# The last four adaLN units among the last key and query units, in memory of their own

## The chip, the cores and the metric

The kernel runs on one core of a Trainium2 chip. The metric is device time in microseconds (us): the median of the runs. Before the change it is 1355.39 us, the median of three runs from 1355.17 to 1358.63. One further execution was profiled; it took 1356.46 us, and every duration below comes from it.

The engines have these names in the profile: PE is TensorE's matrix product, PEld its weight load, DVE is VectorE, ACT is ScalarE, POOL is GpSimd, and SP is SyncE, which here issues nearly all transfers. "SPq" is SyncE's queue of transfer issues.

## The reference, cut to what matters

One layer of a streaming encoder is applied to a prompt of 1024 frames and to a sample of 32 further frames with caches. All is float32.

```python
mod = silu(c) @ w_ada + b_ada                    # per sequence; 1024 -> 6 * 1024
sh1, sc1, g1, sh2, sc2, g2 = split(mod, 6)
h = x * (1 + sc1) + sh1
mq, mk, mv, mo, mi, mf, fq, fk, fv, ff, gu, gv = split(h @ w_in)
hm = mlstm(...)                                  # 4 heads, chunks of 64
hf = forgetting_attention(fq, fk, fv, ...)       # 8 heads, causal, softmax
hg = gu * (lower_triangle(ws) @ layer_norm(gv) + bs)
mix = concat(hm, hf, hg) @ w_o
x = layer_norm(ALPHA * x + (1 + g1) * mix)
h = x * (1 + sc2) + sh2
y = (silu(h @ w_gate) * (h @ w_up)) @ w_down     # 1024 -> 2816 -> 1024
x = layer_norm(ALPHA * x + (1 + g2) * y)
```

The adaLN vector `mod` has six parts of 1024. The last part, `g2`, is used only where the results of `w_down` are added to `x`.

## The kernel before, in words

Everything is held transposed: features on the 128 partitions, frames along the row. Frames are handled in two groups, the first 512 prompt frames (group 0) and the other 512 with the 32 sample frames (group 1). Precise products are made from a rounded high part and a low part of each operand: `weights` (line 104) loads a raw weight tile, lets ScalarE copy it to `whi` (line 116) and VectorE subtract to `wlo` (line 117); `gemm` (line 123) then makes three matmuls for each 128 rows of depth (lines 129 to 131). Raw weight tiles stand in a ring of RAW = 3 buffers, `whi` and `wlo` in rings of WB = 3.

The adaLN vector is made in 24 units of 256 columns. `ada` (line 183) handles one unit: `ada_load` issues two loads of 512 KB, the halves of its weight; `ada_parts` makes eight small float32 matmuls, each with a 32-column operand on the stationary side, in four groups of 32 output partitions (line 201; the trace has 16 records of them for each unit), half 0 first and half 1 added to it. ScalarE copies the result out (line 204), TensorE transposes it twice (line 209), VectorE sums four strips (line 211), and `ada_end` writes the columns of `mod`. The unit holds one PSUM bank from its first matmul to the reduction. Units 0 to 7 are made with the first projection products in `fm_first`, units 16 to 19 and 8 to 15 among the heads by `more`, in a ring of two buffers named "late". Units 20 to 23 are `g2`.

The middle of the kernel, where the change is, runs in this order in the text of `run`: the output projection of group 0 in two ranges of 256 frames (`wo_range`), where the split weights of its units 3 to 5 are kept for the second range in a pool `pw` of 24 KB for each partition, which is closed then; the first layer norm of group 0 (`ln1`), whose mean and variance use the two PSUM banks of the pool `pt`; the key and query units of the heads 5, 6 and 7 for group 1 (`fm_unit` with `evac_qk`), three weight tiles with two ranges of 272 columns each; the mixers of group 1 (attention, mLSTM and the sample's attention, `mixers`); and the feed-forward tiles of group 0 (`up`, then `down`). PSUM is shared out as three banks `pg` for products, two banks `pt` for transposes and sums, and three more for the mixers. Before, each of the feed-forward tiles 0 to 3 is followed by one adaLN unit, 20 to 23, whose two loads take two of the three raw buffers and whose products stand in a `pg` bank.

The order in which each engine runs its instructions is not that of the text. A planner simulates the program with estimated durations and lets each engine take the instruction that stands first in the text among those that are ready; what comes out is a fixed order for each engine, and each engine, and SyncE's queue of issues too, then follows its order strictly. Some stretches are tied by hand: `tie` (line 98) keeps the mixers' first instructions behind certain feed-forward products. A buffer of a closed pool may be written again when the last reader of the tile that stood there is done.

Of the kernel before, what the change touches and what calls it, by code (L numbers as in the profile page):

```python
# [34 lines left out]
PRE = 5  # L35
# [8 lines left out]
RAW = 3  # L44
# [11 lines left out]
def weave(*parts):  # L56

    parts = list(parts)
    while parts:
        for p in list(parts):  # L60
            if next(p, parts) is parts:
                parts.remove(p)
# [6 lines left out]
class Kernel:  # L69
# [125 lines left out]
    def ada_parts(self, u, raws, ppool, ptag):  # L195
        self.phase = "ada"
        nc = self.nc
        ps = self.t(ppool, [P, 512], F32, ptag)
        for half, raw in enumerate(raws):
            for k in range(4):  # L200
                nc.tensor.matmul(ps[32 * k:32 * k + 32, :256], self.c32[:, 4 * half + k, :],
                                 raw[:, k * 256:(k + 1) * 256], start=half == 0, stop=half == 1)
        a = self.t(self.pada, [P, 256], F32, "adas", 2)
        nc.scalar.copy(a, ps[:, :256])
        yield
        self.phase = "ada"
        pt = ps[:, 256:512]
        for half in range(2):
            nc.tensor.transpose(pt[:, half * P:(half + 1) * P], a[:, half * P:(half + 1) * P], self.ident)
        m = self.t(self.pada, [P, 4], F32, "adam", 2)  # L210
        nc.vector.tensor_reduce(m.rearrange("p (h j) -> p h j", h=2), pt.rearrange(
            "p (h g j) -> p h j g", h=2, g=4)[:, :, 0:2, :], AX.X, ALU.add)
        self.ada_end(u, m)
# [1274 lines left out]
    def run(self):  # L1488
        nc, tc, d = self.nc, self.tc, self.d
        dr = self.pool("dr", space=DRAM)  # L1490
        t = lambda shape, tag: self.t(dr, shape, F32, tag)
# [36 lines left out]
        w2, w3 = d["w_in"], d["w_in_f"]  # L1528
# [91 lines left out]
            del kept[0], kept[1]  # L1620
            weave(self.wo_range(st, *MM[0][1], (2, 6, 7, 3, 4, 5, 0, 1), kept, pw), self.ln1(0, st, *MM[0][0]))
        weave(self.ln1(0, st, *MM[0][1]))
        for h in range(PRE, 8):
            self.fm_unit(w3[1 + h], self.evac_qk(h, True), (1,))
        self.ln1_res(0)
        s1.close()
        s4 = ExitStack()
# [8 lines left out]
        for g, (j0, nj) in enumerate(GROUPS):  # L1636
            if g == WOB:
                s4.close()
                s3.close()
                self.pu, self.utag = self.pool("pu", 3, space=PSUM), "gu"  # L1640
                pb = self.pb = self.pool("pb", side="right")
                weave(self.up(0, j0 + 1, act, pa, MM[0]))
                self.operand(1, pb)
                with tc.issue_after(self.lastz.ins):
                    self.wo_mix(1, self.KORDER[1])
                stb = self.ln_begin(nc.gpsimd)
                self.wo(1, stb, MM[1], nc.vector, pb)
                self.operand(1, pb)

                def norm():  # L1650
                    for a, b in MM[1]:
                        yield from self.ln1(1, stb, a, b)

                self.sums()

                def fill():
                    for j in range(j0 + 2, j0 + nj):
                        self.sums()
                        yield from self.up(0, j, act, pa, MM[0])

                weave(fill(), norm())
                continue
            for j in range(j0 + (g > 0), j0 + nj + (g < last)):
                weave(self.up(0, j, act, pa, WIDE if 0 < j < GROUPS[-1][0] else MM[0]))
                if j < 4:
                    self.ada(20 + j, self.wp, "raw", RAW, self.pg, "g")
            if g == WOB - 1:
                st = self.ln_begin(nc.gpsimd, sum=False)
                self.down(0, g, act, WIDE, st)
            else:  # L1670
                self.down(0, g, act, WIDE)
# [37 lines left out]
        t = self.t(self.pz, [P, 4, n], F32R, "z0", 1)  # L1709
        w = self.last_weights(((t[:, 0], t[:, 1]), (t[:, 2], t[:, 3])), (2, 3))  # L1710
        act2 = dict(act)
        for half, (a, b) in enumerate(LN[1][::-1]):
# [6 lines left out]
            else:  # L1719
                h, l = (self.t(pb, [P, KT * 272], F32R, f"{x}{a}", 1) for x in ("ah", "al"))  # L1720
# [118 lines left out]
```

## Time and profile before

| | |
|---|---|
| median of the runs | 1355.39 us |
| the profiled execution | 1356.46 us, span 1354.7 us |
| TensorE (PE) busy | 1329.9 us, 98% |
| VectorE (DVE) busy | 996.8 us, 74% |
| ScalarE (ACT) busy | 660.3 us, 49% |
| last key and query units | 419.8 to 438.7 us |
| adaLN units 20 to 23 | first products at 451.2, last at 505.2 us |

The span is the time from the first to the last instruction in the trace. A row of the timeline gives the start, the duration, the engine, the line of the kernel, the operation, the tile written and the tiles read (buffer numbers left out), the shape, and how many; brackets at its end give the idle time of the engine before it and what ended it. Matmul ends are modelled and overlap the next matmul, so the distance from one start to the next tells what a matmul takes of TensorE. A tile's name begins with the phase in which it was made: `fm` for key and query units, `up` and `dn` for feed-forward, `fox` for attention, `wo` for the output projection, `lna` for the first norm, `tm` and `head` for earlier projections.

### The profile page before, as it was taken

The page shows a single profiled execution, that of the slowest core. Times are in us where ns is not written, and L with a number is a line of the kernel's source. Part 1 is how long each engine was busy: PE and PEld are TensorE (multiplying, and loading weights), DVE is VectorE, ACT ScalarE, POOL GpSimd, SP SyncE. Part 2 cuts the span into 40 slices and gives each one's busy share as a digit, 9 for nine tenths or more (in the row PEclk, how much of TensorE's full clock was granted, in tenths as well). Part 3 has the DMA queues.
Part 4 walks back from the last instruction along what each step waited for, and adds up shares of the span by engine and source line. Part 5 has one row for each costly group of instructions (what it writes and reads, how often), then busy time and mean ns, then how long its engine had stood idle before and what let it go on. Part 6 is the DMA issues. An engine that isn't in the chain of part 4 may idle for free.

```text
span 1354.7 us, 25087 instructions
## 1 busy us (share of the span) xinstructions
PE 1329.9 (98%) x9402; PEld 1208.8 (89%) x9402; DVE 996.8 (74%) x2106; ACT 660.3 (49%) x1305; POOL 230.5 (17%) x263
## 2 busy tenths in 40 slices
PE   9999999999999999999999999999999999999996
PEld 6798888998999778888888888999999999999995
DVE  4646665678679578686776766778988887988777
ACT  3423555455436554554455355436754553535355
POOL 0101100143236200000000000273710000000341
PEclk9999999999999999999999999999999999999998
DMA  9594665546464865354334333664696858553321
GB/s 360 187 306 152 170 200 176 176 150 196 143 210 133 225 184 162 103 159 133 117 109 133 102 90 96 216 172 127 174 251 162 215 152 217 146 178 125 94 79 67
DMA packets 120088, 221.70 MB, mean 164 GB/s; under 512 B 18708, under 2 KB 63920, under 8 KB 119968
## 3 DMA queue, kind: packets, MB, share of 16 engines
q1 hardware_dynamic: 112736, 207.55, 48.6%
q0 software_dynamic: 6032, 11.94, 5.3%
q8 instruction: 74, 1.21, 0.3%
q10 hardware_dynamic: 1200, 0.62, 0.2%
q14 instruction: 46, 0.38, 0.1%
HBM read 188.13 MB, written 51.85 MB: 177 GB/s over the span
## 4 chain that ended last, share of the span: by engine, by line
PE 86%; DVE 6%; DMA 4%; ACT 2%; issue 1%; SPq 0%; POOL 0%; ACTq 0%; DVEq 0%; POOLq 0%
PE up_g L129 5%; PE up_g L131 5%; PE up_g L130 5%; PE dn_g L129 4%; PE dn_g L131 4%; PE dn_g L130 4%; PE tm_g L397 3%; PE tm_g L399 3%; PE tm_g L398 3%; PE sup_u L129 3%; PE sup_u L131 3%; PE sup_u L130 3%; PE wo_g L130 2%; PE wo_g L131 2%; PE wo_g L129 2%; PE fox_t L932 2%
## 5 line engine op out<-in xcount | busy, mean ns | idle before, releaser
L129 PE MATMUL up_g<-tm_ah,up_whi 128*128 128x512 f32 (+1 forms) x384 | 140.2, 365 | 1.2 <-ACT up_whi L116 0.6
L130 PE MATMUL up_g<-tm_al,up_whi 128*128 128x512 f32 (+1 forms) x384 | 140.6, 366 | 0.0
L131 PE MATMUL up_g<-tm_ah,up_wlo 128*128 128x512 f32 (+1 forms) x384 | 139.8, 364 | 0.5 <-DVE up_wlo L117 0.5
L1357 ACT CAST sup_whi<-sup_raw 128x1024 fp32r<-128x1024 f32 x54 | 56.0, 1048 | 90.1 <-PE dn_u L130 46.3
L116 ACT CAST up_whi<-up_raw 128x1024 fp32r<-128x1024 f32 x50 | 52.5, 1049 | 66.3 <-PE dn_g L130 25.8
L129 PEld LDWEIGHTS up_g<-tm_ah,up_whi 128*128 128x128 f32 x384 | 72.2, 188 | 13.7 <-ACT up_whi L116 1.1
L131 PEld LDWEIGHTS up_g<-tm_ah,up_wlo 128*128 128x128 f32 x384 | 72.3, 188 | 11.4 <-DVE up_wlo L117 1.0
L130 PEld LDWEIGHTS up_g<-tm_al,up_whi 128*128 128x128 f32 x384 | 72.2, 188 | 10.5
L1188 DVE SCALAR_TENSOR_TENSOR wo_z<-dn_g,start_mod,wo_z 128x512 f32<-128x512 f32 (+4 forms) x120 | 60.2, 520 | 21.4 <-PE dn_g L131 20.5
L117 DVE TENSOR_TENSOR up_wlo<-up_raw,up_whi 128x1024 fp32r<-128x1024 f32 x50 | 67.2, 1344 | 11.8 <-ACT up_whi L116 9.8
L1358 DVE TENSOR_TENSOR sup_wlo<-sup_raw,sup_whi 128x1024 fp32r<-128x1024 f32 x54 | 68.0, 1262 | 10.6 <-ACT sup_whi L1357 10.5
L905 ACT ACTIVATE fox_p<-fox_s,fox_fmx 128x384 f32<-128x384 f32 (+2 forms) x96 | 55.1, 578 | 40.0 <-DVE fox_fmx L903 29.0
L131 PE MATMUL dn_g<-up_acth,dn_wlo 128*128 128x512 f32 (+2 forms) x200 | 73.7, 369 | 0.0
L130 PE MATMUL dn_g<-up_actl,dn_whi 128*128 128x512 f32 (+2 forms) x200 | 73.4, 368 | 0.0
L129 PE MATMUL dn_g<-up_acth,dn_whi 128*128 128x512 f32 (+2 forms) x200 | 73.4, 368 | 0.0
L116 ACT CAST dn_whi<-dn_raw 128x1024 fp32r<-128x1024 f32 (+1 forms) x44 | 42.7, 971 | 56.6 <-PE up_g L130 14.3
L900 DVE TENSOR_REDUCE fox_fmx<-fox_s 128x1 f32<-128x384 f32 (+2 forms) x96 | 52.7, 553 | 19.5 <-PE fox_s L897 18.5
L937 ACT CAST fox_pth<-fox_t 128x512 fp32r<-128x512 f32 (+1 forms) x80 | 41.6, 542 | 46.9 <-PE fox_t L932 44.9
L117 DVE TENSOR_TENSOR dn_wlo<-dn_raw,dn_whi 128x1024 fp32r<-128x1024 f32 (+1 forms) x44 | 49.5, 1125 | 16.4 <-ACT dn_whi L116 16.0
L397 PE MATMUL tm_g<-tm_whi,start_h1h 128*128 128x256 f32 (+1 forms) x192 | 55.9, 291 | 1.8 <-DVE tm_traw L468 1.7
L398 PE MATMUL tm_g<-tm_wlo,start_h1h 128*128 128x256 f32 (+1 forms) x192 | 55.8, 291 | 0.0
L399 PE MATMUL tm_g<-tm_whi,start_h1l 128*128 128x256 f32 (+1 forms) x192 | 55.6, 290 | 0.0
(690 smaller groups left out, 4766.7 us busy)
## 6 DMA issues: line engine op xcount, KB each, us to landing
up_raw<-w_gu SPq DMA_DIRECT2D x50, 512.0 KB
dn_raw<-w_dn SPq DMA_DIRECT2D x28, 512.0 KB
ada_late<-w_ada SPq DMA_DIRECT2D x24, 512.0 KB
sup_raw<-w_gu SPq DMA_DIRECT2D x20, 512.0 KB
start_dp<-w_gu SPq DMA_DIRECT2D x19, 512.0 KB
start_dp<-w_gu POOLq DMA_DIRECT2D x19, 512.0 KB, 8.0
wo_raw<-w_o SPq DMA_DIRECT2D x18, 512.0 KB
sup_raw<-start_dp SPq DMA_DIRECT2D x18, 512.0 KB
```

The source lines that it names most:

```text
L116: nc.scalar.copy(hi[:, :w], raw[:, :w])
L117: (eng or nc.vector).tensor_tensor(lo[:, :w], raw[:, :w], f(hi[:, :w]), ALU.subtract)
L129: nc.tensor.matmul(ps, hi, xh(k), start=start and k == 0, stop=False)
L130: nc.tensor.matmul(ps, hi, xl(k), start=False, stop=False)
L131: self.lastmm = nc.tensor.matmul(ps, lo, xh(k), start=False, stop=stop and k == n - 1)
L397: nc.tensor.matmul(ps[:, :ncol], xh, hi, start=k == 0, stop=False)
L398: nc.tensor.matmul(ps[:, :ncol], xh, lo, start=False, stop=False)
L399: nc.tensor.matmul(ps[:, :ncol], xl, hi, start=False, stop=k == 7)
L905: nc.scalar.activation(pr[:, lo:hi], banks[x][:, :hi - lo], AF.Exp, bias=mxs[:, 0:1], accum_out=sums[:, x:x + 1])
L1188: self.lastz = self.nc.vector.scalar_tensor_tensor(z[:, m, x:y], ps[:, x - a:y - a], g[i], z[:, m, x:y], ALU.mult, ALU.add)
L1357: nc.scalar.copy(h, x)
L1358: tt(l, x, f(h), ALU.subtract)
```

## The change

The four units 20 to 23 leave the feed-forward tiles. Units 20 and 21 stand behind the key and query unit of head 5, unit 22 behind that of head 6, and unit 23 behind that of head 7. Their loads go to a pool `pq` of six buffers "late", 24 KB for each partition, in the memory that `pw` had; their products stand in the two banks of `pt`. And for all units from 8 on, half 1, which is loaded last, is now multiplied first.

```diff
-        for half, raw in enumerate(raws):
+        for i, half in enumerate((0, 1) if ptag == "t" and u < 8 else (1, 0)):
             for k in range(4):
                 nc.tensor.matmul(ps[32 * k:32 * k + 32, :256], self.c32[:, 4 * half + k, :],
-                                 raw[:, k * 256:(k + 1) * 256], start=half == 0, stop=half == 1)
+                                 raws[half][:, k * 256:(k + 1) * 256], start=i == 0, stop=i == 1)
...
-        for h in range(PRE, 8):
-            self.fm_unit(w3[1 + h], self.evac_qk(h, True), (1,))
+        with ExitStack() as s7:
+            pq = self.pool("pq", ctx=s7)
+            for u, h in enumerate(range(PRE, 8)):
+                self.fm_unit(w3[1 + h], self.evac_qk(h, True), (1,))
+                for u in (20, 21) if u == 0 else (21 + u,):
+                    self.ada(u, pq, "late", 6, self.pt, "t")
         self.ln1_res(0)
...
                 weave(self.up(0, j, act, pa, WIDE if 0 < j < GROUPS[-1][0] else MM[0]))
-                if j < 4:
-                    self.ada(20 + j, self.wp, "raw", RAW, self.pg, "g")
```

## The prediction

> **What bounds the kernel now.** I read the page first (span, busy shares, the chain), then the busy time by stretches around the change, then TensorE's own rows in the stretch where the four units now stand.
>
> ```profile
> span 1354.7 us, 25087 instructions
> ```
> ```profile
> PE 1329.9 (98%) x9402; PEld 1208.8 (89%) x9402; DVE 996.8 (74%) x2106; ACT 660.3 (49%) x1305; POOL 230.5 (17%) x263
> ```
> ```profile
> PE 86%; DVE 6%; DMA 4%; ACT 2%; issue 1%; SPq 0%; POOL 0%; ACTq 0%; DVEq 0%; POOLq 0%
> ```
>
> TensorE is busy 98% of the span and holds 86% of the chain that ended last. So an edit is worth what it takes from TensorE's own work or from TensorE's waits, and nothing else. The stretches (first column is the window in us, then its length, busy time of each engine, granted clock, DMA share, GB/s):
>
> ```profile
> 408.00:426.00 18.00, 18.00 (x153) 18.00 (x152) 18.00 (x33) 10.85 (x22) 13.32 (x9) 1.00 0.19 58
> 426.00:439.00 13.00, 13.00 (x103) 12.90 (x103) 11.09 (x21) 9.47 (x21) 5.79 (x5) 1.00 0.77 222
> 439.00:470.00 31.00, 29.25 (x194) 23.85 (x193) 18.02 (x36) 17.56 (x41) 8.75 (x10) 1.00 0.81 216
> 470.00:505.00 35.00, 33.94 (x213) 25.95 (x211) 23.07 (x55) 17.51 (x36) 0.18 (x1) 1.00 0.65 190
> 505.00:560.00 55.00, 55.00 (x321) 45.01 (x321) 42.37 (x92) 28.04 (x62) 1.19 (x3) 1.00 0.52 153
> ```
>
> The last key and query units run at about 420 to 439 us, where TensorE has no idle time. The first feed-forward tiles run from 439, and there TensorE is idle 31 - 29.25 = 1.75 us up to 470 and 35 - 33.94 = 1.06 us up to 505, together 2.81. After that it is full again. That is the whole idle time that can be won near the change.
>
> **The change part by part.** First what the four units do to the tiles they stand between. These are TensorE's waits from 439 to 470 us (start, duration, the idle time before and what ended it in brackets):
>
> ```profile
> 448.19 0.38 PE L129 MATMUL up_g<-tm_ah,up_whi 128*128 128x256 f32 x1 [0.59 <-DVE up_sil L1288]
> ...
> 467.79 0.50 PE L129 MATMUL up_g<-tm_ah,up_whi 128*128 128x512 f32 x1 [0.63 <-ACT up_whi L116]
> ...
> 469.05 0.50 PE L131 MATMUL up_g<-tm_ah,up_wlo 128*128 128x512 f32 x1 [0.53 <-DVE up_wlo L117]
> ```
>
> They add up to 1.75, all that is idle there. The second and third are one late weight tile. Its way back, in SyncE's queue and on ScalarE:
>
> ```profile
> 458.28 1.67 SPq L86 DMA_DIRECT2D ada_raw<-w_ada  x2
> 460.04 0.38 SPq L86 DMA_DIRECT2D up_raw<-w_gu  x1
> ```
> ```profile
> 466.69 1.04 ACT L116 CAST up_whi<-up_raw 128x1024 fp32r<-128x1024 f32 x1 [0.57 <-DMA up_raw<-w_gu]
> ```
>
> The load of the feed-forward weight goes out directly behind two adaLN loads, which use two of the three "raw" buffers that it needs too. ScalarE then waits for it, and TensorE waits for ScalarE and VectorE. With the adaLN loads gone from this ring and this queue, the load goes out at least 460.04 - 458.28 = 1.76 us sooner, which covers 0.63 + 0.53 = 1.16. Term one: -1.16, between 0 (if the ring turns no sooner) and -1.16. What is late next is the softmax of the attention, and TensorE has feed-forward products to do meanwhile.
>
> Second, the products. One unit is 8 small matmuls (16 records); here three of the four:
>
> ```profile
> 451.21 0.63 PE L201 MATMUL ada_g<-ada_raw,start_c 128*32 128x256 f32 x4
> ...
> 452.25 1.06 PE L201 MATMUL ada_g<-ada_raw,start_c 128*32 128x256 f32 x12
> ```
> ```profile
> 483.91 1.07 PE L201 MATMUL ada_g<-ada_raw,start_c 128*32 128x256 f32 x16
> 484.91 0.50 PE L129 MATMUL up_g<-tm_ah,up_whi 128*128 128x512 f32 x1
> ```
> ```profile
> 499.29 1.05 PE L201 MATMUL ada_g<-ada_raw,start_c 128*32 128x256 f32 x10
> 500.27 0.38 PE L940 MATMUL fox_o<-fox_ptl,fox_v 128*128 128x256 f32 x1
> ...
> 505.00 0.63 PE L201 MATMUL ada_g<-ada_raw,start_c 128*32 128x256 f32 x6
> 505.56 0.51 PE L129 MATMUL dn_g<-up_acth,dn_whi 128*128 128x512 f32 x1
> ```
>
> An undivided unit takes 484.91 - 483.91 = 1.00 us of TensorE from start to next start. The divided one takes 0.98 + 0.56 = 1.54, so dividing costs 0.54. The other divided one shows the same in durations, 0.63 + 1.06 against 1.07, so I give it the same 0.54. They are divided because attention work, written earlier than the units and so ahead of them, comes in between. After the change the units are written before that work. Term two: 2 x -0.54 = -1.08, between 0 (other work comes between) and -1.08. The Trainium skill, "TensorEngine Tiling (Array Packing)", section "Key Properties", says that changing the tiling mode drains TensorE; these units are 32 columns wide, all around them is 128, so each division would add a drain. The trace agrees with a price of 0.54. Nothing in the sum needs that rule.
>
> Third, the reversed halves. The change also lets the twelve units between the first eight and these four begin with the half that lands last, so the wait comes before the first product rather than in the middle. One of them before:
>
> ```profile
> 76.92 0.64 PE L201 MATMUL ada_t<-ada_late,start_c 128*32 128x256 f32 x8
> ```
> ```profile
> 78.55 0.64 PE L201 MATMUL ada_t<-ada_late,start_c 128*32 128x256 f32 x8
> ```
>
> That is 0.64 + 0.64 - 1.07 = 0.21 in durations. The divided unit above shows 1.05 + 0.63 - 1.07 = 0.61 in durations for 0.54 in starts, so 0.07 is overlap, and 0.14 is left. Term three: -0.14 for this one. Upper end: two more divisions of the dear kind saved, -1.08. Lower end: 0; no unit in this stage waits for its load on TensorE long enough to matter, and later start of the next load into the two buffers moves by one unit, 1 us.
>
> Fourth, the wait of 0.59 at 448.19. VectorE has this before the operation waited for:
>
> ```profile
> 446.77 0.91 DVE L996 MEMSET foxs_k<- 2x1024 f32 x1 [0.27 <-DVE tm_al L1235]
> 447.71 0.42 DVE L1288 TENSOR_TENSOR up_sil<-up_g,up_sil 128x256 f32<-128x256 f32 x1
> ```
>
> After the change TensorE comes to this place up to four units, 4 us, later, while VectorE's norm work before it has not moved by as much. The wait may go or stay; I take half. Term four: -0.30, between 0 and -0.59.
>
> Now what moves. TensorE's 4 x 1.00 us and its eight transposes are the same at either place: 0. The evacuation moves to ScalarE and VectorE at 420 to 445, and the loads move with it:
>
> ```profile
> L204 ACT COPY ada_adas<-ada_g x4: 367/370/380, 453.4 to 508.0; 128x256 f32<-128x256 f32 x4
> L211 DVE TENSOR_REDUCE ada_adam<-ada_g x4: 155/162/169, 462.5 to 511.4; 128x4 f32<-128x16 f32 x4
> ```
> ```profile
> ada_raw<-w_ada SPq DMA_DIRECT2D x8, 512.0 KB
> ```
>
> ScalarE gets 4 x 0.37 = 1.5 us and VectorE 4 x 0.16 plus the three tiny column operations of each unit. VectorE is full from 408 to 426 (18.00 of 18) and has 1.9 us left up to 439, but TensorE takes 4 us longer over the same stretch, so I count 0; if that cover is gone, the norm that feeds the first feed-forward tile is late by these operations, under 2 us. The eight loads are 8 x 0.52 = 4.2 MB. The DMA share is 0.19 from 408 to 426, so six of them have room there; the place they leave had 0.81. The Trainium skill, "DMA: Bandwidth & Descriptors", section "Issuing engines are not separate DMA queues", has all transfers share the same 16 engines, so by it a load that is moved only collides somewhere else; here the shares say that the new place is emptier. On SyncE the eight issues come ahead of feed-forward weights and of the stores of keys and queries. The first six wait for buffers that the output projection's units 3 to 5 held, free by about 414 us; the last two wait for the products of unit 20, and behind them stand those stores and loads. I take 0 for that, since TensorE waits for no load in 408 to 439 now. The bank moves from the three of the products to the two of the transposes: see the slower rival.
>
> The sum: -1.16 - 1.08 - 0.14 - 0.30 = -2.68. Durations are from an execution of 1356.46 us (span 1354.7 and 1.76 around it), 1.07 above the median of 1355.39. On the median the forecast is 1355.39 - 2.68 = 1352.7.
>
> **The rivals.** The rows for them, waits of TensorE and SyncE (us in total, times, longest), and single operations:
>
> ```profile
> PE ada_t L209 <- ACT ada_adas L204: 0.6, 1, 0.6
> ```
> ```profile
> PE tm_g L397 <- DVE tm_traw L468: 1.7, 1, 1.7
> ```
> ```profile
> SPq L86 <- DVE up_wlo L117: 13.3, 7, 4.0
> ```
> ```profile
> 462.45 0.17 DVE L211 TENSOR_REDUCE ada_adam<-ada_g 128x4 f32<-128x16 f32 x1
> ```
> ```profile
> 419.79 0.29 PE L129 MATMUL fm_g<-start_h1h,fm_whi 128*128 128x272 f32 x1
> ```
> ```profile
> 438.74 0.28 PE L129 MATMUL up_g<-tm_ah,up_whi 128*128 128x256 f32 x1
> ```
>
> Better than forecast: the order of everything behind the change is planned anew, and the whole 2.81 us idle from 439 to 505 goes, with -1.08 for divisions there and -1.08 in the early stage. That is -4.97, so 1350.4. For it: without the adaLN loads the weight ring runs further ahead. Against it: 1.06 of the idle belongs to the mixers, whose chain the change does not touch. The longest wait of TensorE on another engine is 1.7, in the stage of the twelve early units; if the new order also loses that one, 1348.7.
>
> It does not do what it says: SyncE waits 13.3 us for VectorE's split (from 372 to 520 us), which frees the weight ring, so the ring itself, not the adaLN loads, may keep the feed-forward weight late; and the units may be divided again by key and query products. Then terms one and four are 0: 1355.39 - 1.08 - 0.14 = 1354.2, or with no term at all 1355.4.
>
> Slower: the two transpose banks. A unit holds its bank from its first product to the reduction, at 451.21 to 462.45 plus 0.17, so 11.4 us. Unit 22 needs the bank of unit 20, and a key and query unit's products take (438.74 - 419.79) / 3 = 6.3 us. If the order puts unit 22 one such unit behind unit 20, TensorE stands still 11.4 - 6.3 = 5.1 us, and the time is 1355.39 - 2.68 + 5.1 = 1357.8, no more than within 0.3%. VectorE is busier there, 11.09 of 13 (0.85) against 18.02 of 31 (0.58); an estimate of the hold from that is 11.4 x 0.85 / 0.58 = 16.7, the wait 10.4, the time 1363.1. It decides from a hold of 6.3 + 2.68 + 4.07 = 13.1 us. Against it: units that use these banks wait on TensorE for ScalarE's copy only once, 0.6, in the whole trace, and the order is planned with such holds.
>
> **How the numbers follow.** 0.3% of 1355.39 is 4.07, about what a measurement of this kernel can tell from no change: faster means under 1351.3, slower over 1359.5. Forecast 0.38 (its own range 1351.2 to 1354.2, 0.06 of the chance under 1351.3); better 0.32, all under 1351.3; no effect 0.14; slower 0.16. So faster 0.38, same 0.46, slower 0.16. The range goes from 1348.7, all gains with the early wait, to 1359.0, which takes in the 5.1 us wait and leaves out most of the slower case and a little below.
>
> **What would show it.** Right: no wait for up_whi or up_wlo on TensorE in the first two feed-forward tiles; adaLN products as 16 records in one piece; TensorE without idle time in the key and query units. Wrong: idle time on TensorE ahead of an adaLN product or transpose between 420 and 450, named for a load, the bank's reduction or ScalarE's copy; or new waits far from the change, from the new order.

## The result, and the profile after

The changed kernel is faster: the ratio of its time to that of the kernel before is 0.9976, 95% interval 0.9965 to 0.9987 (medians 1352.48 us and 1356.67 us, 11 runs each). That is 0.24%, within the 0.3% that the prediction counts as the same. On the 1355.39 us of the first three runs the ratio makes 1352.1 us. The profiled execution took 1351.69 us with a span of 1349.8 us. Measured again beside another kernel, the ratio was 0.9985, 0.9973 to 0.9997.

The page after (span, busy shares, chain):

```profile
span 1349.8 us, 25092 instructions
```
```profile
PE 1326.0 (98%) x9402; PEld 1207.2 (89%) x9402; DVE 992.0 (73%) x2106; ACT 658.6 (49%) x1305; POOL 227.6 (17%) x263
```
```profile
PE 88%; DVE 5%; DMA 3%; ACT 1%; issue 1%; SPq 1%; DVEq 0%; ACTq 0%
```

The same stretches as before, with the window first, then its length and the busy time of PE, PEld, DVE, ACT and POOL, the granted clock, the DMA share and GB/s:

```profile
408.00:426.00 18.00, 18.00 (x151) 18.00 (x151) 18.00 (x34) 11.53 (x21) 13.31 (x9) 1.00 0.69 242
426.00:439.00 13.00, 13.00 (x111) 10.84 (x110) 11.44 (x22) 8.79 (x21) 5.01 (x5) 1.00 0.90 254
439.00:470.00 31.00, 31.00 (x218) 27.08 (x217) 20.36 (x48) 20.15 (x43) 5.32 (x9) 1.00 0.77 227
470.00:505.00 35.00, 35.00 (x199) 28.37 (x198) 25.67 (x53) 17.57 (x38) 0.53 (x1) 1.00 0.45 121
```

All 2.81 us of idle time on TensorE between 439 and 505 us are gone: 31.00 of 31 and 35.00 of 35. The loads have gone into the empty place: the DMA share rose from 0.19 to 0.69 at 408 to 426 us and fell from 0.65 to 0.45 at 470 to 505. SyncE's queue shows how (start, time in issue, what is loaded from where):

```profile
408.38 0.33 SPq L86 DMA_DIRECT2D up_raw<-w_gu  x1
408.81 6.51 SPq L86 DMA_DIRECT2D ada_late<-w_ada  x6
422.08 0.33 SPq L86 DMA_DIRECT2D up_raw<-w_gu  x1
425.08 0.33 SPq L86 DMA_DIRECT2D up_raw<-w_gu  x1
428.10 0.33 SPq L86 DMA_DIRECT2D up_raw<-w_gu  x1
```

Six adaLN loads go out together, and by 428 us four feed-forward weight tiles have been asked for, where before there were two by 423 us and then an adaLN load in their place.

To see where the time came from, I cut the span at the first product of the early projections (`tm_g`), the first of the output projection of group 0 (`wo_g`) and the first of the later feed-forward products (`sup_u`). The rows of after that answer this (durations in ns, then first and last start in us):

```profile
L397 PE MATMUL tm_g<-tm_whi,start_ah x192: 277/281/397, 60.0 to 292.3; 128*128 128x256 f32 x128, 128*128 128x264 f32 x64
```
```profile
L129 PE MATMUL wo_g<-tm_ah,wo_whi x128: 276/281/468, 369.4 to 418.7; 128*128 128x256 f32 x128
```
```profile
L129 PE MATMUL sup_u<-wo_ah,sup_whi x144: 282/287/292, 996.2 to 1293.6; 128*128 128x272 f32 x144
```

In the kernel before these first starts are 61.6, 369.1 and 1000.9 us. The three parts, in us, for every profiled execution of this study, one for each row; the last column is explained below the table:

| kernel | `tm` to `wo` | `wo` to `sup` | `sup` to end | stretches at half clock (first, second part) |
|---|---|---|---|---|
| before | 307.5 | 631.8 | 353.8 | 1, 1 |
| changed | 309.4 | 626.8 | 353.6 | 1, 0 |
| changed, measured again | 309.8 | 625.1 | 353.6 | 1, 0 |
| half 0 first in units 8 to 19 | 307.3 | 626.4 | 354.0 | 1, 0 |
| the same, measured again | 306.7 | 626.4 | 354.1 | 0, 0 |
| half 0 first in all units (move alone) | 308.4 | 627.0 | 353.8 | 1, 0 |
| half 0 first in units 8 to 19, last units one, one, two | 308.1 | 626.5 | 353.7 | 1, 0 |
| before, reversed halves only | 308.7 | 631.9 | 353.6 | 1, 1 |
| changed, loads in the raw ring | 310.3 | 639.4 | 354.4 | 1, 3 |
| changed, two buffers | 307.7 | 632.6 | 353.5 | 0, 1 |
| before, undivided in place | 308.4 | 635.3 | 353.6 | 1, 2 |
| half 0 first in units 8 to 19, products in the product banks | 307.9 | 634.8 | 353.9 | 1, 2 |
| before, without the four units | 308.4 | 626.3 | 353.7 | 1, 0 |

So the middle part is 5.0 us shorter and the early part 1.9 us longer. Not all of the 5.0 us is the change. TensorE's granted clock is 1.00 nearly everywhere, but there are stretches of about 3.4 us in which it is 0.50 (one twice or three times as long counts as two or three). The kernel before has such a stretch at 374 us, ahead of the units that were moved; there the changed kernel ran at full clock, and so did six of the seven other executions with half 0 first in units 8 to 19, so the stretch does not belong to the code (before, then changed):

```profile
374.00:376.00 2.00, 2.00 (x12) 2.00 (x12) 1.44 (x2) 0.26 (x1) 0.00 (x0) 0.50 1.08 377
374.00:376.00 2.00, 2.00 (x19) 2.00 (x18) 1.78 (x3) 0.11 (x1) 0.35 (x1) 1.00 1.06 393
```

Eighteen products of the output projection take 3.64 us there in the kernel before (from 373.93) and 2.15 us in the changed one (from 373.77), so one stretch at half clock costs about 1.5 us, and about 3.5 of the 5.0 us are won by the change. In the early part both executions have one such stretch, so the 1.9 us stand. The 1.6 us by which `tm_g` starts sooner (60.0 against 61.6) are no effect of the change either: up to there the code is the same, and the two executions that start at 61.6 and 61.5 us are the ones with half clock at about 9 to 12 us; the other eleven start at 59.4 to 60.0.

The loss in the early part has a row. TensorE's order there, with the idle time before in brackets:

```profile
86.62 1.07 PE L201 MATMUL ada_t<-ada_late,start_c 128*32 128x256 f32 x16 [1.54 <-DMA ada_late<-w_ada]
```

In the kernel before, no adaLN unit after the first eight waits on TensorE for a load.

### The profile page after: what moved, and what is told of

The parts are those of the page before. It is cut to its first block, busy times and chain, and to the rows that moved or that the text cites. A ratio compares the mean times of both kernels' runs of the same rounds, so it can differ in the third digit from the quotient of the medians.

```text
span 1349.8 us, 25092 instructions
## 1 busy us (share of the span) xinstructions
PE 1326.0 (98%) x9402; PEld 1207.2 (89%) x9402; DVE 992.0 (73%) x2106; ACT 658.6 (49%) x1305; POOL 227.6 (17%) x263
## 4 chain that ended last, share of the span: by engine, by line
PE 88%; DVE 5%; DMA 3%; ACT 1%; issue 1%; SPq 1%; DVEq 0%; ACTq 0%
PE up_g L129 6%; PE up_g L130 6%; PE up_g L131 6%; PE dn_g L129 4%; PE dn_g L131 4%; PE dn_g L130 4%; PE tm_g L397 3%; PE sup_u L131 3%; PE sup_u L129 3%; PE sup_u L130 3%; PE tm_g L399 3%; PE tm_g L398 3%; PE fox_t L932 2%; PE wo_g L129 2%; PE wo_g L131 2%; PE wo_g L130 2%
## 5 line engine op out<-in xcount | busy, mean ns | idle before, releaser
L117 DVE TENSOR_TENSOR up_wlo<-up_raw,up_whi 128x1024 fp32r<-128x1024 f32 x50 | 63.4, 1267 | 12.7 <-ACT up_whi L116 11.7
L900 DVE TENSOR_REDUCE fox_fmx<-fox_s 128x1 f32<-128x384 f32 (+2 forms) x96 | 52.8, 553 | 19.1 <-PE fox_s L897 18.1
L938 DVE TENSOR_TENSOR fox_ptl<-fox_t,fox_pth 128x512 fp32r<-128x512 f32 (+1 forms) x80 | 49.9, 632 | 7.9 <-ACT fox_pth L937 7.4
```

Source lines behind the costliest of these rows:

```text
L117: (eng or nc.vector).tensor_tensor(lo[:, :w], raw[:, :w], f(hi[:, :w]), ALU.subtract)
L900: nc.vector.tensor_reduce(mxs[:, x:x + 1], s[:, :w], AX.X, ALU.max, negate=True)
```

## The experiments

**Half 0 first again in the early units.** The changed kernel, with the reversed halves for the last four units only.

```diff
-        for i, half in enumerate((0, 1) if ptag == "t" and u < 8 else (1, 0)):
+        for i, half in enumerate((0, 1) if u < 20 else (1, 0)):
```

> The changed kernel, but units 8 to 19 multiply half 0 first again; only 20 to 23 keep half 1 first. Theory (the gain is won wholly between 419 and 505 us, and the reversed halves cost in the early stage): TensorE's wait of 1.54 us for an adaLN load at 86.6 us goes, the key and query stretch starts about 0.9 us sooner after the first tm product than in the changed kernel, and the time is 0.5 to 1.5 us under the changed kernel's, a ratio to the kernel before of about 0.997. Rival (the reversed halves are part of the gain): the early units are divided again, 0.14 to 0.54 us each, and the time is equal to the changed kernel's or up to 1.5 us over it.

Measured: ratio to the kernel before 0.9962 (0.9948 to 0.9977), median 1350.58 us. TensorE's longest waits between 61 and 420 us no longer name an adaLN load:

```profile
PE tm_g L397 <- DVE tm_traw L468: 1.9, 1, 1.9
PE wo_g L129 <- ACT wo_qs L1053: 0.7, 1, 0.7
```

The early part is back at 307.3 us, and the middle keeps its gain. To have both kernels on one chip I ran it again beside the changed kernel.

> The same kernel as in the first experiment (the changed kernel with half 0 first in units 8 to 19), beside the changed kernel on the same chip. Theory (reversed halves cost a wait of 1.5 us in the early stage): 1 to 2 us faster than the changed kernel run beside it. Rival (early halves make no difference): within 0.5 us of it.

> The changed kernel again, beside the kernel above. Both theories expect about 3 us under the kernel before, as measured first, a ratio of 0.9965 to 0.9987.

Measured: 0.9979 (0.9970 to 0.9988) with half 0 first, median 1351.32 us; 0.9985 (0.9973 to 0.9997) for the changed kernel, median 1353.57 us. The intervals overlap, so the times alone do not settle that the first is faster. The idle time of TensorE in the early part does point one way. It was 3.9 to 5.1 us in the eight executions with half 0 first in units 8 to 19 and 5.9 to 7.0 us in the five with half 1 first, all of which have the wait for an adaLN load, of 1.1 to 2.4 us.

**Reversed halves alone.** The kernel before with the new order of the halves, nothing moved.

```diff
-        for half, raw in enumerate(raws):
+        for i, half in enumerate((0, 1) if u < 8 else (1, 0)):
             for k in range(4):
...
```

> The kernel before, only with half 1 multiplied first in units 8 to 23; the last four units stay between the feed-forward tiles. Theory (the place and the memory bring the gain): no gain, between 0 and 1.5 us slower than before, by the wait of about 1.5 us at 87 us that the changed kernel has too; attention products still divide the last four units, since they stand ahead of them in the text, and the waits for up_whi and up_wlo stay. Rival (undivided products bring the gain): the last four units are undivided, at least 1.1 us faster than before.

Measured: 1.0006 (0.9994 to 1.0019). No gain, as the theory had it. The longest of TensorE's waits between 420 and 560 us (us in total, times, longest) are those of the kernel before for the late weight tile and the sil, the first of them longer:

```profile
PE up_g L129 <- ACT up_whi L116: 1.1, 1, 1.1
PE up_g L131 <- DVE up_wlo L117: 0.5, 1, 0.5
PE up_g L129 <- DVE up_sil L1288: 0.5, 1, 0.5
```

and in the early part stands the same new wait as in the changed kernel:

```profile
PE ada_t L201 <- DMA ada_late<-w_ada: 1.6, 1, 1.6
```

**The move alone.** The changed kernel with half 0 first everywhere.

```diff
-        for i, half in enumerate((0, 1) if ptag == "t" and u < 8 else (1, 0)):
+        for i, half in enumerate((0, 1)):
```

> The changed kernel with half 0 first in every unit, so the move and the memory alone. Theory (the move and the memory are the whole gain; reversed halves only cost): as the kernel with half 0 first in units 8 to 19, a ratio of 0.996 to 0.998, and no idle time of TensorE for loads between 420 and 505 us. Rival (reversed halves keep the last four units undivided at the new place): 1 us or more over that kernel, with the last four units in two pieces each.

Measured: 0.9976 (0.9965 to 0.9987), median 1351.05 us. The move and the memory are the whole gain. This time alone is no better than that of the changed kernel, though the early units have half 0 first again; what their order costs shows only over all runs (term three below). The last four units are cut exactly as in the changed kernel, three in one piece and one in two, so the reversed halves do nothing for them.

**The new place, but the raw ring.** The changed kernel, with the loads of the last four units in the ring they had before.

```diff
-                    self.ada(u, pq, "late", 6, self.pt, "t")
+                    self.ada(u, self.wp, "raw", RAW, self.pt, "t")
```

> The changed kernel, but the last four units take their loads in the ring of three raw buffers, as before, at the new place among the key and query units. Theory (what counts is that they leave the feed-forward tiles; the ring is free enough among the key and query units): as the changed kernel, 3 to 4 us faster than before. Rival (the memory of their own is what makes the new place possible): eight loads of 512 KB pass through the ring between the key and query weights and the first feed-forward weights, at about 2.2 us each one by one, so the first feed-forward tile is late; TensorE waits 3 us or more between 420 and 470 us for up_whi or for adaLN loads, and the gain is gone or the kernel is slower than before.

Measured: 1.0068 (1.0042 to 1.0093), slower than before. The rival was right: without memory of their own the new place costs more than the old one. The windows and the waits of TensorE there:

```profile
420.00:439.00 19.00, 12.97 (x97) 10.06 (x96) 16.19 (x33) 11.71 (x25) 11.91 (x9) 0.83 0.50 161
```
```profile
PE ada_t L201 <- DVE start_mod L221: 3.3, 1, 3.3
PE ada_t L209 <- ACT ada_adas L204: 1.3, 2, 0.8
PE fox_s L897 <- DMA fox_k<-start_dql: 0.9, 1, 0.9
PE ada_t L201 <- DVE lna_tmp L1091: 0.9, 1, 0.9
PE up_g L129 <- ACT up_whi L116: 0.9, 1, 0.9
PE up_g L131 <- DVE up_wlo L117: 0.8, 1, 0.8
PE fm_g L129 <- ACT fm_whi L116: 0.5, 1, 0.5
```

TensorE is idle 6.03 of 19 us. My expectation named the wrong waits, though: TensorE waits mainly not for the loads but for the transpose bank (3.3 us until the column operations of the unit before are done, 0.9 until the norm lets go) and the copy, probably since with the key and query weights pushed back there is no other work in between. Three stretches at half clock follow this idle time, so the whole loss is more than the waits.

**The changed kernel with two buffers instead of six.**

```diff
-                    self.ada(u, pq, "late", 6, self.pt, "t")
+                    self.ada(u, pq, "late", 2, self.pt, "t")
```

> The changed kernel, but the memory of the last four units is two buffers instead of six. Theory (what counts is that the loads are out of the raw ring): the loads of a unit wait for the products of the one before it, on SyncE and with the feed-forward weights behind them in the queue; TensorE waits for adaLN loads or first feed-forward weights, 1 to 5 us of the gain are lost, but not the whole loss of the raw ring variant, so a ratio of 0.998 to 1.003. Rival (it is enough to have any memory apart): as the changed kernel, 0.9965 to 0.9987.

Measured: 1.0027 (1.0017 to 1.0037). Near the change there is one wait, for an adaLN load, and between 840 and 920 us a second one, in group 1's output projection:

```profile
PE ada_t L201 <- DMA ada_late<-w_ada: 1.9, 1, 1.9
```
```profile
PE wo_g L129 <- ACT up_ah L1128: 3.2, 1, 3.2
```

So the price of few buffers at their own place is 1.9 us, and 3.2 us stand 400 us later, where the kernel before waits for nothing, followed by a stretch at half clock. The planner seems to have laid the mixers out differently: the last attention transpose starts at 840.0 us here and at 835.1 us in both the kernel before and the changed one. The time lies in the range that I had written, but it is no clean price of the buffers.

**Undivided in the old place.** The kernel before, products of the last four units ahead of the attention work in the planner's order, half 1 first for them.

```diff
...
-                    self.ada(20 + j, self.wp, "raw", RAW, self.pg, "g")
+                    raws = self.ada_load(20 + j, self.wp, "raw", RAW)
+                    with tc.high_priority(2000):
+                        for _ in self.ada_parts(20 + j, raws, self.pg, "g"):
+                            pass
```

> The kernel before, with the last four units in their old place and in the raw ring, but their products ahead of the attention work in the planner's order and begun with the half that lands last, so that each stands in one piece. Theory (the terms of the prediction's sum): the two divisions go, -1.1 us; the waits for up_whi, up_wlo and up_sil, 1.75 us together, stay, so the ratio is about 0.9992. Rival (undivided products are the greater part of the gain): 0.998 or less. Rival (products held back until both halves are there stand in front of other work): new waits of TensorE for adaLN loads between 439 and 505 us, ratio 1.000 to 1.002.

Measured: 1.0040 (1.0026 to 1.0054). All four units ran in one piece and it did not help. TensorE's waits from 439 to 520 us:

```profile
PE fox_s L896 <- DMA fox_qp<-start_dql: 4.2, 1, 4.2
PE up_g L129 <- ACT up_whi L116: 0.7, 1, 0.7
PE up_g L129 <- DVE up_sil L1288: 0.5, 1, 0.5
PE ada_g L201 <- DMA up_raw<-w_ada: 0.3, 1, 0.3
```

The waits for the late weight and for the sil stay, as the theory had it; the new 4.2 us belong to the loads of the next head's attention. They went out behind three weight loads of the down projection issued together, where the kernel before has one directly ahead of them:

```profile
491.71 2.22 SPq L86 DMA_DIRECT2D dn_raw<-w_dn  x3
494.02 1.14 SPq L86 DMA_DIRECT2D fox_k<-start_dqh  x2
495.25 0.55 SPq L86 DMA_DIRECT2D fox_qp<-start_dqh  x1
495.84 0.65 SPq L86 DMA_DIRECT2D fox_qp<-start_dql  x1
```

None of the three cases I had written for this run held, and the 4.2 us were followed by two stretches at half clock; the price of a division could not be read from its time.

**Without the four units.** The kernel before with `g2` left out: its columns of `mod` are set to 1.

```diff
+        nc.vector.memset(self.mod[:, 20:24], 1.0)
...
-                if j < 4:
-                    self.ada(20 + j, self.wp, "raw", RAW, self.pg, "g")
```

> The kernel before without the last four units: the columns of mod for g2 are set to 1, so this part of adaLN is left out. It gives the floor under every place of the four. Theory (the four cost their own TensorE time plus the waits and divisions read from the trace): 4 x 1.00 for products, 4 x 0.14 for transposes, 2 x 0.54 for divisions, 0.63 + 0.53 for the late weight tile and 0.59 for the late sil, 7.4 us in all, so a ratio of 0.9945; the changed kernel would then stand about 4 us over the floor. Rival (the gain of the change is in the new order of the mixers and the feed-forward tiles rather than in these waits): the floor is under 5 us below before, and TensorE is still idle 2 us or more between 439 and 505 us.

Measured: 0.9976 (0.9958 to 0.9994), where 0.9945 was expected, though the idle time between 439 and 505 us fell from 2.81 to 1.03 us. The rest went into waits between 820 and 920 us, again in group 1's output projection:

```profile
PE wo_g L129 <- ACT up_ah L1129: 1.6, 1, 1.6
PE wo_g L129 <- DVE wo_z L1189: 1.3, 1, 1.3
```

From the first `tm_g` (59.5 us) to the end this execution took 1347.9 - 59.5 = 1288.4 us against 1293.1 before, 4.7 less. About 1.5 of that is the half clock at 374 us, which only the kernel before has, so 3.2 us are left, and with the 2.9 us of these two waits it would have been 6.1, under the 7.4 expected. The price list is not confirmed by it: the wait for the sil, for one, is still there, 0.8 us.

**Products in the three product banks.** On top of the first experiment:

```diff
-                    self.ada(u, pq, "late", 6, self.pt, "t")
+                    self.ada(u, pq, "late", 6, self.pg, "g")
```

> The changed kernel with half 0 first in units 8 to 19, and the products of the last four units in the three banks for products instead of the two for transposes. Theory (TensorE never waits for the transpose banks, since the planner knows when they come free): the place of the products moves by some us, no wait is won, the time is within 2 us of the kernel with the transpose banks. Rival (the two transpose banks delay the units, and three banks would free them): the units' excess of about 1 us between 419 and 445 us goes and the ratio is under 0.9965. Rival on the other side (a unit that holds a product bank for 11 us takes it from key and query products): TensorE waits 2 us or more for a product bank between 420 and 450 us, ratio 1.000 or more.

Measured: 1.0004 (0.9992 to 1.0017): the gain is gone. The units run undivided, but key and query products and the first feed-forward tile now wait:

```profile
PE fm_g L129 <- ACT start_qks L493: 1.5, 2, 1.1
PE up_g L129 <- DVE ada_adam L211: 0.3, 1, 0.3
```
```profile
PE wo_g L129 <- ACT up_ah L1128: 2.5, 1, 2.5
```

The third case, a product bank taken away, is what the first two rows show, with 1.8 us rather than 2 or more; the third row is the wait in group 1's output projection once more, again with a stretch at half clock behind it.

**One, one, two.** On top of the first experiment:

```diff
-                for u in (20, 21) if u == 0 else (21 + u,):
+                for u in (20 + u,) if u < 2 else (22, 23):
```

> The changed kernel with half 0 first in units 8 to 19, and unit 20 behind the first key and query unit, 21 behind the second, 22 and 23 behind the third. Theory (the units are planned into TensorE's free order wherever they stand among the key and query units): within 1 us of two, one, one; a ratio of 0.996 to 0.998. Rival (the distribution matters through the transpose banks): more than 1.5 us either way, with a wait or a division in the units' rows to show for it.

Measured: 0.9969 (0.9959 to 0.9980), median 1350.60 us. It makes no difference that shows: the second unit is cut in the same way, by the transposes of the first.

## Why the prediction was right

The forecast was 1352.7 us, a gain of 2.68 on 1355.39. The measured ratio makes 3.2 us of it (1.8 to 4.7 by its interval) and the second measurement 2.0 (0.4 to 3.7), so the total came out, and so did the likeliest class, within 0.3%. The mechanism of the main term was right. But that the total lies so near is in part luck, since two errors of opposite sign stand behind it: the middle part won about 3.5 us where the sum has 2.54, and the early part lost about 1.5 us where the sum has a gain of 0.14. The rows of the four terms come from places at full clock, so the stretches at half clock do not touch them.

*Term one, the late weight tile, -1.16: right.* Neither wait is left between 420 and 560 us. The two experiments that left the loads in the raw ring and between the feed-forward tiles (reversed halves alone, undivided in place) kept waits there, 1.6 and 0.7 us; the one that took the ring along to the new place lost 7.6 us in the middle part. So leaving the ring is needed at the new place. Whether memory of their own would have been enough at the old place was not tried. The rival by which the ring itself keeps the weight late is refuted.

*Term two, the divisions, -1.08: half.* The four units now (TensorE, 431 to 447 us):

```profile
431.57 1.07 PE L201 MATMUL ada_t<-ada_late,start_c 128*32 128x256 f32 x16
...
435.53 0.62 PE L201 MATMUL ada_t<-ada_late,start_c 128*32 128x256 f32 x2
436.08 0.44 PE L209 MATMUL ada_t<-start_ident,ada_adas 128*128 128x128 f32 x2
436.44 1.06 PE L201 MATMUL ada_t<-ada_late,start_c 128*32 128x256 f32 x14
...
441.39 1.07 PE L201 MATMUL ada_t<-ada_late,start_c 128*32 128x256 f32 x16
...
445.35 1.07 PE L201 MATMUL ada_t<-ada_late,start_c 128*32 128x256 f32 x16
```

Two divisions became one, by the transposes of unit 20 itself. At 0.54 each this is -0.54, not -1.08.

*Term three, the reversed halves, -0.14: wrong.* I said that no unit of the early stage waits for its load long enough to matter, and set the lower end at 0. The order did make the units at 77, 140 and 173 us whole, but it cut the one at 214 us in two, and the one at 87 us now waits 1.54 us for the half that lands last. That wait had no place in my sum. In the kernel before, the loads of that unit went out 17.5 and 19.1 us behind the weight load that opens this stage, in the changed kernel both 19.4 us behind it, one directly after the other. Whether this alone makes the wait is not shown.

What this costs shows best in runs of equal mean granted clock, over all runs that have it on record, from several chips. At 0.996 the kernel before took 1354.6 us on average (22 runs), the changed kernel 1351.7 (11), and the kernels with half 0 first in units 8 to 19 that kept the move, the six buffers and the transpose banks 1350.7 (16, from four experiments). At 0.995 it was 1355.6 (26), 1353.9 (9) and 1351.7 (9). So the reversed halves cost 1.0 to 2.2 us where I had written a gain, and the move without them is worth 3.9 us.

*Term four, the wait for the sil, -0.30: the whole 0.59 went.* The two attempts in the old place kept it at 0.5 us, and without the four units it was 0.8. So it seems to be covered, as I had argued, by the 4 us of products that now stand ahead of it.

*What I left out.* "1.06 of the idle belongs to the mixers, whose chain the change does not touch" was wrong too. These two waits of the kernel before are gone:

```profile
502.21 0.67 PE L738 MATMUL mlstm_s<-mlstm_mqb,mlstm_mqk 128*128 128x256 f32 x2 [0.80 <-issue]
503.15 0.33 PE L940 MATMUL fox_o<-fox_ptl,fox_v 128*64 128x256 f32 x1 [0.27 <-DVE fox_ptl L938]
```

In this the rival "better than forecast" was right. Of the 3.5 us that the middle part won, 2.81 are idle time and 0.54 a division, 3.35 together; the rest is within what these readings can tell. Why the mixers wait no longer is not shown: their order was planned anew.

*The slower rival* did not happen, since a unit holds its transpose bank for less time at the new place: from 431.57 us to the end of the reduction at 437.19 us, 5.8 us, against 11.4 us before.

```profile
437.19 0.17 DVE L211 TENSOR_REDUCE ada_adam<-ada_t 128x4 f32<-128x16 f32 x1
```

My estimate of 16.7 us, by VectorE's busy share, went the wrong way. In the kernel before the transposes came 4.3 us after the copy was done, in TensorE's order behind other products, and the reduction another 4.0 us later, because VectorE stood idle ahead of it, for a load of the mixers:

```profile
461.62 0.69 DVE L732 TENSOR_TENSOR mlstm_mw<-mlstm_mb,start_maskbig 128x512 f32<-128x512 f32 x1 [4.86 <-DMA mlstm_mb<-start_dM]
```

So the fixed orders made the hold long, not a full VectorE. The mechanism itself exists; in the raw ring variant TensorE waited 3.3 us for it. One thing was uneven in the chances: with a wait of 5.1 us this rival comes to 1357.8, within 0.3% by the prediction's own sum, yet all of its 0.16 was counted as slower.

## What to carry to other kernels

Side work that borrowed a buffer ring of the main stream delayed the main stream here by its loads. It paid to give it memory of its own at a place where the queue and the DMA engines had room, and to ask for most of it at once. The new place needs the memory: the same place with the borrowed ring cost 0.7%. Where a planner fixes the order, look at the whole trace after a local edit: three variants here kept part or most of the local gain and lost 2.5 to 3.2 us at a stage 400 us later. And before you look for a cause of the last 1.5 us between two executions, compare the granted clock along both.

## What the runs showed of the hardware that I had not expected

The price of dividing the 32-column products is not mainly a price of switching, as I had taken it with the Trainium skill ("TensorEngine Tiling (Array Packing)", "Key Properties"), which says that changing the tiling mode drains TensorE. Of one unit's 16 records, 2, 4, 6 or 8 in one piece took 0.62 to 0.64 us in the kernel before and the changed one, and 10, 12, 14 or 16 took 1.05 to 1.07. Eight records are one round of the four groups of output partitions. So the sizes fit a count of rounds: a cut in the middle of a round makes a third round, 0.54 us from start to start, while a cut between the rounds (the unit at 77 us, 0.57 twice against 1.00) costs 0.14. A price of the switch alone should be the same at either place; by this reading the trace leaves at most 0.14 for it.

Idle time on TensorE was followed by a lower granted clock: where it was idle 6.03 of 19 us, in the raw ring variant, the granted clock was 0.83 on average, and 1.00 in the same window of the kernel before. Seen in windows of 2 us, the clock is 0.50 for 3.4 us at a time: 3.4 us behind the waits of 1.24 and 0.34 us at 372 to 374 us in the kernel before, 6.8 us behind the wait of 4.2 us in the variant undivided in place, and 10.2 us in the raw ring variant (estimates from the means of these windows, taking the clock as 1.00 or 0.50). So a wait can cost some 1.5 us more than its own length. Not every wait has this behind it: at 372 to 374 us the changed kernel waited 0.76 and 0.34 us, and the kernel without the four units waited 1.6 and 1.3 us between 820 and 920 us, and both stayed at 1.00. What decides it is not shown.
